# A three-block layer on one core: where the low parts of plain gate weights come from, and five reorderings beside it

## The chip, the core and the metric

The kernel runs on one core of a Trainium2 chip. The core has a matmul engine (TensorE, PE in the profile, with its weight loads as PEld), three engines for elementwise work (VectorE = DVE, ScalarE = ACT, GpSimd = POOL), a SyncE (SP) that here only issues DMA transfers, and 16 DMA engines. The metric is the device time of one execution in microseconds (us).

## The reference

One layer of a model over 2048 prompt tokens and 64 sample tokens, all in float32, model width 1024. Cut to what matters:

```python
h = rms_norm(x, g_pre)
vA, bA, cA, zA, q, f, iv, zB, gA, gB = split_cols(h @ w_in)      # ten outputs of 1024 columns
u = cA * vA                                                       # path A
yA = (silu(zA) * bA * causal_conv3(conv_hist ++ u, conv_w)) @ w_a_out
S_new, o = hgrn2_scan(S0, silu(q) * scale, 1 - fg, iv, log(fg))   # path B: 8 heads, chunks of 64
yB = (head_norm(o) * g_onorm * silu(zB)) @ w_b_out
merged = sigmoid(gA) * yA + sigmoid(gB) * yB
x = x + rms_norm(merged @ w_o, g_post)
gate = sigmoid(rms_norm(x, g_ple) @ w_ple_gate)
x = x + (p @ w_ple_proj) * gate
return x, new_conv, S_new
```

## The kernel before

The 2112 tokens are cut into three blocks of 768, 704 and 640 (the sample tokens end block 1), called block 0, 1 and 2 here. A block is worked in two halves of 384, 352 and 320 columns. Activations lie with the 1024 features over 8 row tiles of 128 partitions (k = 0 to 7), tokens along the free axis.

**Precision.** Every operand is split into a high part (a cast, on ACT) and a low part (value minus high part, on DVE; function `split`, L207). A product takes three matmuls: high by high, high by low, low by high. They stand in L382 to L384 for the groups below, in L516 to L518 for `in_turn`, in L549 to L551 for plain products (`mm3`).

**Groups of seven products.** `sgroup` makes two output tiles (128 output columns each, called i1 and i2) for both halves of a block with seven products instead of eight, each over 4 k: 7 x 4 x 3 = 84 matmuls. The products take, in this order, the weights A11, S3, S1, S2, A12, A22, S4 (the table PRODUCTS). A11, A12 and A22 are plain blocks of the weight matrix; S1 to S4 are sums and differences of its blocks. Results pass through banks `pg`; L396 copies a bank to an `hf` tile, L402, L407, L422 and L429 add such pieces on DVE.

**Where weights come from.** Block 0 loads plain blocks (`load_raw`, L217, queue SP), computes the sums on DVE (L316), splits both (L207), and stores the sums (L295) and the low parts (L244, tensor `low`) to DRAM. Blocks 1 and 2 load everything through SP, in program order: for each weight the raw tile (L217), whose high part ACT casts (L237), and the low part (L238). `kept_w` does this for one weight, `combined` for a group. Tiles rotate: 5 of `raw`, 4 of `hi`, 4 of `lo`, 3 of `s`. `low_tile` deals out tiles for loaded lows by a counter: three of seven lie in an `s` tile, four in a `lo` tile. A load waits on SP until the tile that it is to fill has been read by PE, and what is queued behind it on SP waits too.

**Order in a block.** First the groups of the gates gA and gB (`gates`; in blocks 1 and 2 the first seven of them run ahead, woven into the norm at the end of the block before). Then path B (`path_b`): for each of 8 heads two groups (`head_prep`), and pieces of the attention of the head before (`head_attn`, L951 to L1029), which are put in between products through a list of hooks, one taken after each product of a group. Then path A (`path_a`): for j from 0 to 7 two groups each, followed by DVE work such as L808, L827 and L840; at the top of each j it takes a step of a side job (`side`). Then the outputs: block 0 with plain products, blocks 1 and 2 with `in_turn`; W_O of blocks 0 and 1 is made in `final_out` by plain products. Its first two output tiles are made together in `gemm_late`: for each tile and half, all k but one (`late`: 7 in block 0, 3 in block 1), then the late k of all four. Last come the norm (`final_norm`) and the operands of the next block.

**The side job for sums.** `prepare_sums` makes the four sums of each group of W_O (in block 1) and W_G (in block 2) ahead: it loads four blocks through the POOL queue (L339), computes S1, S3, S2, S4 on DVE (L356, L358, L360, L362), stores each (L345), splits it (L207) and stores its low (L348). From j = 3 on, each j takes one step: the four sums of one group, and then the loads of the next.

**Norms.** `col_rstd` turns sums of squares into a factor per token, for each half: transposes on PE (L640), a reduction on DVE (L642), scale and offset on DVE (L611), a power on POOL (L613); `spread` brings the columns back over all partitions by transposes (L624). `rms` does it for both halves, one after the other.

The order on each engine comes from a scheduler that follows program order with priorities (`tc.high_priority`, `placed` and `behind_all` change it).

Of the kernel before, what the change touches and what calls it, by code (L numbers as in the profile page):

```python
# [83 lines left out]
def hybrid_step(  # L84
# [147 lines left out]
    def split_w(raw, key=None, queue=SP):  # L232

        hi = wp.tile([P, 4, P], F32R, tag="hi", name=nm("hi"))
        if key in lows:
            lo = low_tile()
            A.copy(hi, raw)  # L237
            SP.dma_start(lo.bitcast(F32), lows[key])  # L238
            return hi, lo
# [58 lines left out]
    def kept_w(i1, i2, name, anew=False):  # L298
# [4 lines left out]
        return split_w(load_raw(sums[i1][name]), (i1, name))  # L303

    def combined(i1, i2, first):

        queue = SP if first else G
        with tc.high_priority():
            if not first and i1 in sums:
                return {n: kept_w(i1, i2, n) for _, n, _, _, _ in PRODUCTS}  # L310
            a11, a21, a22, a12 = (load_raw(w_blk[i, h]) for i, h in ((i1, 0), (i2, 0), (i2, 1), (i1, 1)))
            out = dict(A11=split_w(a11, (i1, 0), queue))
# [10 lines left out]
            out["A12"] = split_w(a12, (i1, 1), queue)  # L323
            out["A22"] = split_w(a22, (i2, 1), queue)
# [3 lines left out]
    def prepare_sums(firsts, ahead):  # L328
# [23 lines left out]
        for n, (i1, _) in enumerate(groups):  # L352
# [3 lines left out]
            V.tensor_tensor(a22, a21, a22, ALU.add)  # L356
            keep("S1", i1, a22)
            V.tensor_tensor(a21, a11, a21, ALU.subtract)  # L358
            keep("S3", i1, a21)
            V.tensor_tensor(a11, a22, a11, ALU.subtract)  # L360
            keep("S2", i1, a11)
            V.tensor_tensor(a12, a12, a11, ALU.subtract)  # L362
            keep("S4", i1, a12)
            if not ahead and n + 1 < len(groups):
                nxt = load(*groups[n + 1])
            yield

    def sgroup(i1, i2, hc, sink, first, mid=None, by_k=False):
# [17 lines left out]
        if by_k:  # L386
            for k in range(KH):
                for n in range(4):
                    product(n, (k,))
# [41 lines left out]
    def plain_group(i1, i2, hs, sink, raws=None, between=None):  # L431
# [4 lines left out]
        def split_of(c, h):  # L436
            key = ((i1, i2)[c], h)
            raw = raws[c, h] if raws else load_raw(w_blk[key])
            with nullcontext() if raws else tc.high_priority():
                w[c, h] = split_w(raw, key)  # L440
# [126 lines left out]
    def gemm_late(idxs, act, segs, late):  # L567
# [3 lines left out]
        ks = [k for k in range(KB) if k != late] + [late]  # L571
# [44 lines left out]
    def cols_tile(n):  # L616
        return small.tile([P, (n + P - 1) // P], F32, tag=f"cols{n}", name=nm("cols"))
# [16 lines left out]
    def col_rstd(acc, n):  # L634

        pc = ps_attn()
        cols = cols_tile(n)
        with placed():
            for i, o in tiles_of(n):
                T.transpose(pc[:, i * P : i * P + P], acc[:, o : o + P], ident)  # L640
        nt = cols.shape[1]
        V.tensor_reduce(cols, cols3(pc, nt), axis=mybir.AxisListType.X, op=ALU.add)  # L642
        rstd_of(cols, cols, 1.0 / D)
        return cols

    def rms(acc, out, segs, copy=A.copy):


        cols = [col_rstd(acc[:, cols_of(sg)], sg["n"]) for sg in segs]
# [881 lines left out]
```

## Time and profile before

| | us |
|---|---|
| median of three runs | 2614.24 (2612.5 to 2616.74) |
| the profiled execution | 2618.3 |
| its span | 2616.6 |
| TensorE busy | 2584.3 (99%) |
| VectorE busy | 1648.8 (63%) |
| ScalarE busy | 1525.9 (58%) |
| GpSimd busy | 376.6 (14%) |
| moved by DMA | 747.01 MB, 285 GB/s in the mean |

How to read it. A busy share counts the time in which an instruction of the engine is under way, so 99% on PE does not say that PE runs at its peak: matmuls are pipelined, and a late operand or a lower granted clock shows in how many start in a stretch. A group's row gives line, engine, operation, tiles (output, then inputs), count, busy time and mean of one in ns, then the idle time ahead and what ended it. In the list of waits a row says which line stood, for what, how long in all, how often, and the longest. Times in windows count from the start of the span. Block 0 lasts until about 900 us, block 1 until about 1760; path B of block 2 lies between about 1900 and 2150, its path A from about 2150 to 2305.

### The profile page before, as it was taken

The page shows a single profiled execution, that of the slowest core. Times are in us where ns is not written, and L with a number is a line of the kernel's source. Part 1 is how long each engine was busy: PE and PEld are TensorE (multiplying, and loading weights), DVE is VectorE, ACT ScalarE, POOL GpSimd, SP SyncE. Part 2 cuts the span into 40 slices and gives each one's busy share as a digit, 9 for nine tenths or more (in the row PEclk, how much of TensorE's full clock was granted, in tenths as well). Part 3 has the DMA queues.
Part 4 walks back from the last instruction along what each step waited for, and adds up shares of the span by engine and source line. Part 5 has one row for each costly group of instructions (what it writes and reads, how often), then busy time and mean ns, then how long its engine had stood idle before and what let it go on. Part 6 is the DMA issues. An engine that isn't in the chain of part 4 may idle for free.

```text
span 2616.6 us, 47076 instructions
## 1 busy us (share of the span) xinstructions
PE 2584.3 (99%) x16432; PEld 2564.4 (98%) x16432; DVE 1648.8 (63%) x3165; ACT 1525.9 (58%) x2908; POOL 376.6 (14%) x698
## 2 busy tenths in 40 slices
PE   8999999999999999999999999999999999999999
PEld 8999999999999999999999999999999999999999
DVE  8687788788757655445554557845344444568776
ACT  6666576554433564567775546546677755556746
POOL 1000000110144021210011221002100000211110
PEclk9999999999999999999999999999999999999999
DMA  7677677788788698876768998859977779999977
GB/s 274 220 262 265 232 247 263 274 302 268 267 330 286 233 379 284 279 242 223 229 224 296 364 381 304 305 167 377 366 252 244 245 254 332 381 335 359 344 264 264
DMA packets 362095, 747.01 MB, mean 285 GB/s; under 512 B 44513, under 2 KB 49153, under 8 KB 361857
## 3 DMA queue, kind: packets, MB, share of 16 engines
q1 hardware_dynamic: 319680, 579.81, 64.2%
q0 software_dynamic: 41888, 164.15, 17.2%
q8 instruction: 129, 2.11, 0.3%
q14 instruction: 110, 0.89, 0.1%
q10 hardware_dynamic: 288, 0.05, 0.0%
HBM read 532.26 MB, written 211.57 MB: 284 GB/s over the span
## 4 chain that ended last, share of the span: by engine, by line
PE 82%; DMA 5%; ACT 4%; DVE 3%; issue 2%; POOL 1%; ACTq 0%; POOLq 0%; SPq 0%; DVEq 0%
PE pg L382 16%; PE pg L383 16%; PE pg L384 16%; PE pg L551 5%; PE pg L550 5%; PE pg L549 5%; PE pg L516 4%; PE pg L517 4%; PE pg L518 3%; DMA raw<-S 2%; DMA r<-w_blk 1%; PE pa L984 1%; PE pa L1020 1%; PE pa L970 1%; ACT hi L237 1%
## 5 line engine op out<-in xcount | busy, mean ns | idle before, releaser
L382 PE MATMUL pg<-r,hi 128*128 128x320 f32 (+2 forms) x3304 | 1087.5, 329 | 5.5 <-DVE r L429 3.8
L383 PE MATMUL pg<-r,hi 128*128 128x320 f32 (+2 forms) x3304 | 1069.3, 324 | 0.0
L384 PE MATMUL pg<-r,lo 128*128 128x384 f32 (+2 forms) x2356 | 766.9, 326 | 4.1 <-DMA lo<-low 4.1
L237 ACT CAST hi<-raw 128x512 fp32r<-128x512 f32 x720 | 442.9, 619 | 465.5 <-PE pg L383 137.2
L382 PEld LDWEIGHTS pg<-r,hi 128*128 128x128 f32 x3304 | 622.6, 188 | 7.9 <-issue 4.7
L383 PEld LDWEIGHTS pg<-r,hi 128*128 128x128 f32 x3304 | 622.7, 188 | 0.2 <-DVE r L207 0.2
L384 PEld LDWEIGHTS pg<-r,lo 128*128 128x128 f32 x2356 | 443.2, 188 | 5.1 <-DMA lo<-low 5.1
L384 PE MATMUL pg<-r,s 128*128 128x352 f32 (+1 forms) x948 | 299.3, 316 | 1.0 <-DMA s<-low 1.0
L549 PE MATMUL pg<-r,hi 128*128 128x384 f32 (+1 forms) x768 | 256.1, 334 | 1.6 <-ACT r L207 1.6
L550 PE MATMUL pg<-r,hi 128*128 128x384 f32 (+1 forms) x768 | 256.1, 334 | 0.1
L207 ACT CAST hi<-raw 128x512 fp32r<-128x512 f32 x218 | 134.7, 620 | 178.2 <-PE pg L550 57.9
L207 DVE TENSOR_TENSOR r<-r,r 128x320 fp32r<-128x320 f32 (+7 forms) x298 | 182.0, 633 | 64.9 <-ACT r L207 63.9
L551 PE MATMUL pg<-r,lo 128*128 128x384 f32 (+1 forms) x656 | 219.9, 335 | 0.0
L517 PE MATMUL pg<-r,hi 128*128 128x320 f32 (+1 forms) x672 | 211.1, 316 | 0.2 <-DVE r L207 0.2
L516 PE MATMUL pg<-r,hi 128*128 128x320 f32 (+1 forms) x672 | 206.0, 316 | 0.9 <-ACT r L207 0.8
L207 DVE TENSOR_TENSOR lo<-raw,hi 128x512 fp32r<-128x512 f32 x218 | 149.3, 686 | 63.1 <-ACT hi L207 60.4
L207 ACT CAST r<-r 128x320 fp32r<-128x320 f32 (+7 forms) x298 | 161.0, 576 | 46.0 <-DVE r L715 12.7
L207 ACT CAST hi<-s 128x512 fp32r<-128x512 f32 x160 | 98.0, 618 | 145.7 <-PE pg L383 130.8
L384 PEld LDWEIGHTS pg<-r,s 128*128 128x128 f32 x948 | 178.5, 188 | 1.8 <-DMA s<-low 1.8
L396 ACT COPY hf<-pg 128x352 f32<-128x352 f32 (+2 forms) x354 | 156.7, 444 | 3.8 <-PE pg L384 3.6
L207 DVE TENSOR_TENSOR lo<-s,hi 128x512 fp32r<-128x512 f32 x160 | 110.1, 689 | 68.9 <-ACT hi L207 67.3
L549 PEld LDWEIGHTS pg<-r,hi 128*128 128x128 f32 x768 | 144.8, 189 | 2.2 <-ACT r L207 2.2
(365 smaller groups left out, 4097.7 us busy)
## 6 DMA issues: line engine op xcount, KB each, us to landing
raw<-w_blk SPq DMA_DIRECT2D x570, 256.0 KB, 4.2
lo<-low SPq DMA_DIRECT2D x411, 256.0 KB, 4.6
raw<-S SPq DMA_DIRECT2D x408, 256.0 KB, 4.4
low<-lo SPq DMA_DIRECT2D x314, 256.0 KB, 3.5
s<-low SPq DMA_DIRECT2D x309, 256.0 KB, 4.5
S<-s SPq DMA_DIRECT2D x152, 256.0 KB, 3.2
r<-w_blk POOLq DMA_DIRECT2D x64, 256.0 KB, 6.8
S<-r POOLq DMA_DIRECT2D x64, 256.0 KB, 5.8
```

The costliest lines, as they stand in the source:

```text
L207: return A.copy(hi, src).ins, V.tensor_tensor(lo, src, hi.bitcast(F32), ALU.subtract).ins
L237: A.copy(hi, raw)
L382: add(hi[:, k, :], xhi, start=start and k == 0, stop=False)
L383: add(hi[:, k, :], xlo, start=False, stop=False)
L384: last[0] = add(lo[:, k, :], xhi, start=False, stop=k == KH - 1).ins
L396: copied = A.copy(got[n], ps[bank])
L516: add(hi[:, k, :], xhi, start=start and k == 0, stop=False)
L517: add(hi[:, k, :], xlo, start=False, stop=False)
L518: last[0] = add(lo[:, k, :], xhi, start=False, stop=k == KH - 1).ins
L549: T.matmul(ps, hi[:, k % 4, :], xhi[:, c], start=k == ks[0], stop=False)
L550: T.matmul(ps, hi[:, k % 4, :], xlo[:, c], start=False, stop=False)
L551: last[0] = T.matmul(ps, lo[:, k % 4, :], xhi[:, c], start=False, stop=k == ks[-1]).ins
```

## The change

It has six parts.

1. In blocks 1 and 2 the low parts of plain blocks (A11, A12, A22) in the groups are no longer loaded: DVE makes them from the loaded raw tile (L207 gets 240 more instructions of 128x512), in `lo` tiles. Block 0 no longer stores them. On SP, lows loaded fall from 720 to 480 (240 fewer), lows stored from 314 to 192 (122 fewer). The lows of S1, S2 and S3 always take an `s` tile; that of S4 is still dealt by the counter.
2. `prepare_sums` for W_O and W_G stops after each sum. For j above 3, the steps run as hooks in path A, at every third product, so that the sums come between the products of a j, not at its top.
3. The first two output tiles of W_O in block 1 take k in the order 4, 5, 6, 7, 0, 1, 2 and then 3 (before 0, 1, 2, 4, 5, 6, 7, then 3). Block 0's order is the same as before.
4. In the first gate group of a block, the four products that go by k run as (A11, S3) for k 0 and 1, (S1, S2) for k 0 and 1, then all four for k 2 and for k 3. Before, all four ran for each k.
5. `col_rstd` takes both halves at once: one L611 and one L613 of six columns instead of two of three.
6. In path B of block 2 the attention pieces of a head start one product later (one more empty hook).

The number of matmuls is the same. Cut to its core:

```diff
-    def split_w(raw, key=None, queue=SP):
+    def split_w(raw, key=None, queue=SP, spare=None):
         hi = wp.tile([P, 4, P], F32R, tag="hi", name=nm("hi"))
         if key in lows:
-            lo = low_tile()
+            lo = low_tile() if spare is None else sum_tile(F32R)
...
-    def kept_w(i1, i2, name, anew=False):
+    def kept_w(i1, i2, name, anew=False, spare=None):
...
-        return split_w(load_raw(sums[i1][name]), (i1, name))
+        return split_w(load_raw(sums[i1][name]), (i1, name), spare=spare)
...
-                return {n: kept_w(i1, i2, n) for _, n, _, _, _ in PRODUCTS}
+                return {n: kept_w(i1, i2, n, True, None if n == "S4" else True) for _, n, _, _, _ in PRODUCTS}
...
-            out["A12"] = split_w(a12, (i1, 1), queue)
-            out["A22"] = split_w(a22, (i2, 1), queue)
+            out["A12"] = split_w(a12)
+            out["A22"] = split_w(a22)
...
+            for name, dst, x, y, op in steps:
+                V.tensor_tensor(dst, x, y, op)
+                keep(name, i1, dst)
+                if name == "S4" and not ahead and n + 1 < len(groups):
+                    nxt = load(*groups[n + 1])
+                if name == "S4" or not ahead:
+                    yield
...
         if by_k:
-            for k in range(KH):
-                for n in range(4):
-                    product(n, (k,))
+            for ns, ks in (((0, 1), (0, 1)), ((2, 3), (0, 1)), ((0, 1, 2, 3), (2,)), ((0, 1, 2, 3), (3,))):
+                for k in ks:
+                    for n in ns:
+                        product(n, (k,))
...
-        ks = [k for k in range(KB) if k != late] + [late]
+        ks = [(late + 1 + k) % KB for k in range(KB)]
...
-        cols = [col_rstd(acc[:, cols_of(sg)], sg["n"]) for sg in segs]
+        cols = col_rstd([acc[:, cols_of(sg)] for sg in segs])
...
-            hooks.extend([None] * 3 if first and hd == 0 else [])
+            hooks.extend([None] * (3 if first and hd == 0 else 1 if bl["last"] else 0))
...
-                if j >= 3:
+                if j == 3:
                     next(sums_, None)
+                elif j > 3 and not first:
+                    hooks.extend([partial(next, sums_, None), None, None] * 4)
```

How the order moves, at three places. PE at the start of W_O in block 1, before (r_4682 is the high part of row 0, r_4683 its low part, r_4689 row 1, r_4696 row 2, r_4755 row 4; L624 are the last transposes of the norm factors):

```order
L624 MATMUL pa_4825_20458<-ident_75,cols_3954_16592 128x128 x3
L549 MATMUL pg_4838_20487<-r_4682_19816,hi_4827_20465 128x352
L550 MATMUL pg_4838_20487<-r_4683_19817,hi_4827_20465 128x352
L551 MATMUL pg_4838_20487<-r_4682_19816,s_4828_20466 128x352
L549 MATMUL pg_4838_20487<-r_4689_19848,hi_4827_20465 128x352
L550 MATMUL pg_4838_20487<-r_4690_19849,hi_4827_20465 128x352
L551 MATMUL pg_4838_20487<-r_4689_19848,s_4828_20466 128x352
L549 MATMUL pg_4838_20487<-r_4696_19880,hi_4827_20465 128x352
```

and now (r_4630 is row 4, r_4637 row 5, r_4644 row 6):

```order
L627 MATMUL pa_4700_20205<-ident_75,cols_3829_16339 128x128 x3
L552 MATMUL pg_4713_20234<-r_4630_19885,hi_4705_20218 128x352
L553 MATMUL pg_4713_20234<-r_4631_19886,hi_4705_20218 128x352
L554 MATMUL pg_4713_20234<-r_4630_19885,s_4706_20219 128x352
L552 MATMUL pg_4713_20234<-r_4637_19914,hi_4705_20218 128x352
L553 MATMUL pg_4713_20234<-r_4638_19915,hi_4705_20218 128x352
L554 MATMUL pg_4713_20234<-r_4637_19914,s_4706_20219 128x352
L552 MATMUL pg_4713_20234<-r_4644_19943,hi_4705_20218 128x352
```

The second half of the weight tile and the rows 4 to 7 come first; rows 0 to 2 follow after 12 matmuls.

DVE in path A of block 2, at the second of the four groups of W_G's sums, before (L407 to L429 are a group's additions; L356 to L362 the four sums; L808 path A's own work):

```order
L407 TENSOR_TENSOR hf_27064<-hf_27064,hf_27079 128x320
L402 TENSOR_TENSOR hf_27049<-hf_27049,pg_27081 128x320
L429 TENSOR_TENSOR r_26990<-hf_27049,hf_27064 128x320
L356 TENSOR_TENSOR r_26984<-r_26983,r_26984 128x512
L358 TENSOR_TENSOR r_26983<-r_26982,r_26983 128x512
L360 TENSOR_TENSOR r_26982<-r_26984,r_26982 128x512
L362 TENSOR_TENSOR r_26985<-r_26985,r_26982 128x512
L429 TENSOR_TENSOR r_26990<-hf_27049,pg_27051 128x320
L808 TENSOR_TENSOR r_26991<-pg_27036,r_26990 128x320
```

and now (the four sums share line L363; L405, L410 and L432 are L402, L407 and L429 of before; the L207 with `raw` is a new split of a plain block's low):

```order
L410 TENSOR_TENSOR hf_26939<-hf_26939,hf_26954 128x320
L363 TENSOR_TENSOR r_26966<-r_26965,r_26966 128x512
L405 TENSOR_TENSOR hf_26924<-hf_26924,pg_26972 128x320
L363 TENSOR_TENSOR r_26965<-r_26964,r_26965 128x512
L207 TENSOR_TENSOR lo_27038<-raw_27035,hi_27037 128x512
L432 TENSOR_TENSOR r_26868<-hf_26924,hf_26939 128x320
L363 TENSOR_TENSOR r_26964<-r_26966,r_26964 128x512
L363 TENSOR_TENSOR r_26967<-r_26967,r_26964 128x512
L432 TENSOR_TENSOR r_26868<-hf_26924,pg_26926 128x320
L845 TENSOR_TENSOR r_26693<-r_26693,r_26868 128x640
```

The sums stand in the second group of a j now, spread among the additions; before, they stood in its first group, all four between two additions.

SP in block 2, before, the loads of a group's weights (S1, S2, A12, A22, S4 by name or `w_blk`; each raw tile is followed by the low of the weight before it):

```order
L238 DMA s_6401_27493<-low_1937_7718 128x512
L217 DMA raw_6405_27502<-S2_1944_7732 128x512
L238 DMA lo_6404_27499<-low_1942_7728 128x512
L217 DMA raw_6408_27508<-w_blk 128x512
L238 DMA s_6407_27505<-low_1947_7738 128x512
L217 DMA raw_6411_27514<-w_blk 128x512
L238 DMA lo_6410_27511<-low_1950_7744 128x512
L217 DMA raw_6414_27520<-S4_1955_7754 128x512
L238 DMA s_6413_27517<-low_1953_7750 128x512
```

and now, in another group of block 2 (s_6385, s_6388 and s_6391 take the lows of this group's S3, S1 and S2; lo_6361 takes the low of the S4 of the group before):

```order
L217 DMA raw_6383_27721<-S3_1951_8005 128x512
L217 DMA raw_6386_27727<-S1_1956_8015 128x512
L238 DMA s_6385_27724<-low_1954_8011 128x512
L217 DMA raw_6389_27733<-S2_1961_8025 128x512
L238 DMA s_6388_27730<-low_1959_8021 128x512
L217 DMA raw_6392_27739<-w_blk 128x512
L238 DMA s_6391_27736<-low_1964_8031 128x512
L238 DMA lo_6361_27588<-low_1930_7877 128x512
L217 DMA raw_6395_27745<-w_blk 128x512
L217 DMA raw_6398_27751<-S4_1970_8043 128x512
```

Only sums have lows to load, and the S4 low of a group stands behind the S2 low of the next.

46 lines of the change are left out of this document (21 added, 25 removed).

## The prediction

> **What bounds the kernel now.** I read the page first, then the busy time by stretches, then what TensorE waited for in each stretch, then the landing times of the transfers.
>
> ```profile
> span 2616.6 us, 47076 instructions
> PE 2584.3 (99%) x16432; PEld 2564.4 (98%) x16432; DVE 1648.8 (63%) x3165; ACT 1525.9 (58%) x2908; POOL 376.6 (14%) x698
> ```
>
> TensorE (PE) is the bound, and the change leaves its number of matmuls as it is. So all that can be won is time in which PE stands or runs slowly, and all that can be lost is new time of that kind. How much there is shows in matmuls started per stretch (the columns are length, then busy time with count of PE, weight loads, DVE, ACT and POOL, then granted clock, DMA share, GB/s):
>
> ```profile
> 500.00:700.00 200.00, 200.00 (x1144) 200.00 (x1144) 164.15 (x274) 97.49 (x187) 17.11 (x35) 1.00 0.84 283
> 1480.00:1560.00 80.00, 79.39 (x493) 79.12 (x492) 44.04 (x81) 41.61 (x82) 19.90 (x47) 1.00 1.03 382
> 1760.00:1830.00 70.00, 65.92 (x437) 64.40 (x437) 37.82 (x63) 44.34 (x85) 15.82 (x27) 0.98 0.99 369
> 2150.00:2200.00 50.00, 50.00 (x344) 50.00 (x343) 19.02 (x33) 24.85 (x47) 2.81 (x8) 1.00 0.93 314
> 2230.00:2300.00 70.00, 65.55 (x431) 64.38 (x430) 36.64 (x63) 33.57 (x67) 16.22 (x34) 0.98 1.04 394
> ```
>
> Undisturbed, a matmul of block 2 (320 columns) starts every 50/344 = 0.145 us; one of block 1 (352 columns) about every 79.4/493 = 0.161 us. At 0.145 us, 482 fit into 70 us. Path A of block 2 (2230 to 2300) has 431, so it loses 51 x 0.145 = 7.4 us; the change from block 1 to 2 (1760 to 1830) has 437 and loses 6.5 us. Both have the DMA share at about 1; the first row, at 0.84 and with DVE busy 82% of the time, loses nothing.
>
> The clock takes part in these losses:
>
> ```profile
> 1698.10:1701.54 3.44, 1.72 (x7) 0.94 (x6) 3.26 (x8) 1.25 (x4) 0.54 (x1) 0.99 0.92 324
> 1701.54:1704.95 3.41, 3.41 (x13) 3.20 (x12) 2.52 (x6) 0.98 (x2) 0.00 (x0) 0.51 0.10 41
> ...
> 1800.50:1803.90 3.40, 1.34 (x9) 1.34 (x10) 1.55 (x3) 0.95 (x2) 1.08 (x2) 1.00 1.03 405
> 1803.90:1807.35 3.45, 3.45 (x15) 3.45 (x14) 1.88 (x3) 2.93 (x5) 0.54 (x1) 0.51 1.04 413
> ...
> 2260.50:2264.00 3.50, 2.20 (x15) 1.94 (x14) 0.00 (x0) 0.62 (x1) 0.00 (x0) 1.00 1.04 410
> 2264.00:2267.50 3.50, 3.10 (x22) 2.84 (x20) 3.09 (x5) 1.25 (x2) 1.66 (x4) 1.00 1.05 392
> 2292.00:2295.46 3.46, 1.62 (x12) 1.39 (x11) 3.32 (x7) 0.62 (x1) 2.17 (x4) 0.99 1.06 393
> 2295.46:2298.87 3.41, 3.41 (x14) 3.41 (x14) 2.23 (x3) 2.85 (x6) 0.18 (x1) 0.51 1.03 405
> ```
>
> Three times a stretch in which PE was busy for only 1.3 to 1.7 of 3.4 us is followed by one at a granted clock of 0.51, with 13 to 15 matmuls where 21 to 24 fit: 1.2 to 1.4 us lost each, 3.9 us in all. A stretch with 2.20 us busy was followed by full clock. So I take it that a wait costs about 1.3 us more once two of them fall close together.
>
> The Trainium skill, "TensorE: Matmul & The Clock Gate", section "HAM oscillation — how this bites in real kernels", sets the bar higher: PE idle for more than about 3.4 us on end. Here the longest waits before the three stretches are near 2 us, so the trace disagrees; by that rule the 3.9 us would not go away with the waits, and the time forecast below would be about 3.9 us longer.
>
> **The change, part by part.**
>
> *W_O of block 1 from k 4 on.* The first output pair reads its left half for all k but one, then its right half. What PE waited for from 1690 to 1900:
>
> ```profile
> PE pg L384 <- DMA lo<-low: 2.2, 1, 2.2
> PE pg L549 <- ACT r L207: 1.6, 2, 1.2
> PE pg L382 <- ACT hf L396: 0.9, 1, 0.9
> PE pg L384 <- DMA s<-low: 0.5, 1, 0.5
> ```
>
> The L549 waits lie at 1698.10 to 1704.95: right halves of the merged rows 0 to 2, which are split last. 20 matmuls started there where 43 fit: 3.7 us lost, 1.3 of it by clock. Starting at k 4 puts 12 matmuls (12 x 0.161 = 1.9 us) ahead of the first late row. The last of the three rows comes some 3.5 us after the first is asked for, so not every wait goes, but what is left is too short for the clock to drop. I take 2.6 us, between 1.2 (waits halved, the clock still drops) and 3.7.
>
> *Plain gate blocks split on chip.* For each of 80 groups in blocks 1 and 2, three loads of a low (256 KB) are replaced by three splits on DVE: 240 loads fewer, and 122 stores in block 0 that are no longer needed. The stores lie where PE loses nothing (500 to 700), so they bring nothing. What a split costs:
>
> ```profile
> L207 DVE TENSOR_TENSOR lo<-raw,hi 128x512 fp32r<-128x512 f32 x218 | 149.3, 686 | 63.1 <-ACT hi L207 60.4 <-DMA low<-lo 1.2 <-ACT r L207 0.9
> ```
>
> 240 x 0.686 = 165 us of DVE, 2.06 us in a group of 84 x 0.145 = 12.2 us: DVE in path A of block 2 goes from 52% to 69%, less than the 82% of 500 to 700. There the same splits ran and PE stood nowhere. I cost them at nothing in steady stretches; their cover is the weights being loaded several products early, and if it is gone a split shows with up to 0.7 us. At the first gate group of a block, where a weight is wanted at once, I charge 0.3 us.
>
> The load on DMA falls by three of 14 weight transfers per group, 3 x 0.262 MB / 12.2 us = 64 GB/s: from 394 to about 330 in path A of block 2. How long a 256 KB transfer takes at such loads, in order 1755 to 1780, 2150 to 2200 (314 GB/s by its row above), 2200 to 2300 and 2300 to 2400 (name, queue, count, size, median us from issue to landing):
>
> ```profile
> DMA packets 3360, 7.00 MB, mean 280 GB/s; under 512 B 404, under 2 KB 404, under 8 KB 3358
> lo<-low SPq DMA_DIRECT2D x7, 256.0 KB, 4.3
> ...
> lo<-low SPq DMA_DIRECT2D x17, 256.0 KB, 3.8
> ...
> DMA packets 18213, 37.91 MB, mean 379 GB/s; under 512 B 2303, under 2 KB 2303, under 8 KB 18206
> lo<-low SPq DMA_DIRECT2D x30, 256.0 KB, 6.8
> ...
> DMA packets 16202, 34.28 MB, mean 343 GB/s; under 512 B 2010, under 2 KB 2026, under 8 KB 16191
> raw<-S SPq DMA_DIRECT2D x29, 256.0 KB, 5.2
> ```
>
> Between 3.8 at 314 and 5.2 at 343 lies 4.6 us at 330: my value, with 3.8 and 6.8 as ends.
>
> *Where the sums' lows lie.* The lows of S1, S2, S3 now always take one of three "s" tiles, S4's one in three groups of seven. After such an S4, the low of the next group's S2 can be issued only when S4's product is done, three products (3 x 12 x 0.145 = 5.2 us, 5.8 in block 1) ahead of its use; 4.6 fits. But SP issues in order. Where S4's low goes to a "lo" tile and is queued behind such an S2, which happens four times in path A of block 2, about 4.0 us are left for it: 4 x 0.6 = 2.4 us lost. At the first gate group of block 2, S1 and S2 wait for tiles that W_O's last lows hold, leaving 3.0 and 3.4 us against 4.3 (first row above): 1.3 + 0.9, of which the second is partly covered by the first; 1.7. Before, each low had six products. This part costs 4.1 us, between 0 and 30 (the slower rival).
>
> *With these, the waits for lows at the change of block.* Of the 6.5 us lost from 1760 to 1830, 9 + 15 matmuls in 1800.50 to 1807.35, where 47 fit, are 3.3 us: one wait of 2.2 for a low and the clock after it. That low is one of a plain block or lies behind them; I take 3.0, with -1 and 5 as ends.
>
> *First gate group in two pairs, one power per norm.* What PE waited for from 896 to 986, the change from block 0 to 1:
>
> ```profile
> PE pg L382 <- ACT hi L237: 0.7, 1, 0.7
> PE pg L384 <- DMA lo<-low: 0.7, 1, 0.7
> PE pa L624 <- POOL cols L613: 0.5, 1, 0.5
> PE pg L384 <- DMA s<-low: 0.5, 1, 0.5
> ```
>
> Taking (A11, S3) for two k before S1 and S2 gives those two weights 12 matmuls instead of 6, 1 us. I take 0.9 of the 1.9 us of weights. The powers:
>
> ```profile
> L613 POOL TENSOR_TENSOR cols<-cols,mhalf 128x3 f32<-128x3 f32 x14 | 14.3, 1028 | 49.7 <-DVE cols L611 49.7
> L613 POOL TENSOR_TENSOR cols<-cols,mhalf 128x1 f32<-128x1 f32 x12 | 8.0, 668 | 47.5 <-DVE cols L611 47.3
> ```
>
> One column 0.67 and three 1.03 give 0.18 a column, so six take about 1.6 against 2 x 1.03 at worst; at most 0.5 us for each norm on the path, with the first half waiting longer and the second less. I take 0.3 for block 0 to 1 and 0.3 for the others; ends -1 and 1.
>
> *One more hook before attention in block 2.* From 1900 to 2150 PE waited seven times (there are eight heads); behind it, one of them in order of time:
>
> ```profile
> PE pa L953 <- DVE r L429: 2.0, 7, 0.3
> ```
>
> ```profile
> 2023.27 0.60 PE L951 MATMUL pa<-ident,r 128*128 128x128 f32 x4
> 2024.19 0.84 PE L953 MATMUL pa<-ident,r 128*128 128x128 f32 x4 [0.33 <-DVE r L429]
> ```
>
> L953 starts 0.92 us after four matmuls that are done in 0.60, and its own four take 0.24 longer than those: 0.3 bare wait, up to 0.32 + 0.24 = 0.6 lost. The attention comes one product (1.74 us) later, more than the wait. DVE now has splits in front of L429, at most three (2.06 us) and mostly one. I take 0.5 x 7 = 3.5 us; ends 0 and 4.2.
>
> *Sums one by one.* Four loads, four sums: before, the loads are issued at one j and DVE stands on them at the top of the next. From 2230 to 2300 on DVE and 2190 to 2300 on PE:
>
> ```profile
> DVE r L356 <- DMA r<-w_blk: 17.8, 3, 6.4
> ```
>
> ```profile
> PE pg L382 <- DVE r L429: 3.2, 3, 1.8
> PE pg L384 <- DMA lo<-low: 1.3, 1, 1.3
> ```
>
> Behind the four sums stands L429, which frees the bank that PE wants. DVE waits of 5 to 6.4 us reached PE with 0.8 to 1.8; so some 4.3 us of it were hidden. Now the sums come half a j later and other work stands between them: the loads have 5 to 6 us, 2 to 3 more than before, and what wait is left on DVE stays under what is hidden. Gone are 3.2 of waits, 1.4 of clock and the restart after each: 5.0 of the 7.4 us; ends 0 and 7.4. In block 1 there is one such wait, 0.3.
>
> **Sum.** 2.6 + 3.0 + 0.9 + 0.6 + 3.5 + 5.0 + 0.3 = 15.9 won, 0.3 + 4.1 lost: 11.5 us net. The profiled execution took 2618.3 us (span 2616.6), which is 4.1 above the median of the runs, 2614.24. 2618.3 - 11.5 - 4.1 = 2602.7, so 2603.
>
> **Rivals.**
>
> *Slower: the short leads meet slow transfers.* If the DMA stays as full as now (it may: what is no longer asked for lets other loads start earlier) and a low takes 6.8 us, it is late by 1.6 in seven groups of path A of block 2, by 1.0 in seven of block 1, by 2.8 for the four S4: 11 + 7 + 11 us; the first gate group adds 2, beyond the 1.7 charged: 31 lost, 2.4 of it charged already. Against this, the 11.5: about 17 us slower, 2631; with 6.2 us in place of 6.8 some 7 slower. It decides from a landing time of about 5.9 us on. For it: 1.04 is a full queue, and 394 GB/s may be what the queue gives, not what is asked. Against it: the 343 GB/s of 2300 to 2400 went with 5.2. 0.17.
>
> *About the same.* A landing time of some 5.3 us costs the S4 lows 3 us more and the first gate group 2; DVE, still late with a sum, keeps 3 of the 5.0 us. Gain 3 to 4: 2611. 0.16.
>
> *More.* All waits named go with their clock, the lows come in time: 3.7 + 5 + 1.9 + 1 + 4.2 + 7.4 - 4 (what else is lost at the change of block and in path A, for which I have no cause) = 19: 2595. For it: landing at 3.8 if 314 GB/s is reached. 0.17.
>
> *Splits and powers in each other's way.* POOL's power could be held up by the added DVE work: then the two norms at the changes of block lose up to 0.69 each and the gains there halve, 3 us less: 2606, inside the forecast's range. The Trainium skill, "SBUF — State Buffer", section "Who interferes with whom", says that a DVE instruction with two SBUF inputs, which a split is, contends with a GpSimd instruction that reads SBUF. From 500 to 700, with DVE at 82%, nothing of PE's time was lost; the rows do not show a held-up power.
>
> **How the numbers follow.** My forecast has 0.50, 2598 to 2608. What a measurement of this kernel can tell from no change is about 0.2%, 5.2 us. Below 2609 lie the forecast and the larger gain: 0.67 faster; 0.16 the same; 0.17 slower. The range from 2593 to 2615 holds the first two and most of the "same" case; outside are the slower rival and a little on either side.
>
> **What the profile after would show.** W_O right: L549 waits under 1 us and no 0.51 near 1702. Sums right: no wait for L429 in path A of block 2, DVE waits on its sums under 4 us each. Hook right: no L953 row. Splits right: DVE near 1810 us, lows in path A landing in 4 to 5 us, DMA share below 1. New waits of L384 for s<-low or lo<-low, over 6 us in sum, or landing times still above 6, would make the prediction wrong; so would splits that PE waits for (L384 <- DVE lo L207).

## The result

The changed kernel is slower: 2631.19 us in the median against 2614.92 of the kernel before, a ratio of 1.0063 with a 95% interval from 1.0044 to 1.0082. The forecast was 2603, with a range from 2593 to 2615. The profiled execution of the changed kernel took 2627.35 us, the fastest of its four; that of before, with 2618.3, lay above its median. So the two traces lie 9 us apart, and the medians 16.

The page of the changed kernel, its span and its busy times:

```profile
span 2625.7 us, 46666 instructions
PE 2581.0 (98%) x16432; PEld 2564.6 (98%) x16432; DVE 1795.0 (68%) x3400; ACT 1528.5 (58%) x2908; POOL 378.3 (14%) x693
```

The number of matmuls is the same, DVE has 146 us more, and PE stands longer. What it waited for, whole execution, the first four rows:

```profile
PE pg L386 <- DMA lo<-low: 16.5, 5, 5.1
PE pg L386 <- DMA s<-low: 7.3, 6, 2.7
PE pa L1089 <- ACT r L207: 6.9, 1, 6.9
PE pa L627 <- POOL cols L616: 3.2, 5, 1.4
```

(L386 is L384 of before, L627 is L624.) Waits for lows were 4.1 + 1.0 us; they are 16.5 + 7.3. The waits for L429's sums, for W_O's operands (L549) and for the attention (L953) are gone. By stretches (896 to 986 is the change from block 0 to 1, 1690 to 1712 the start of W_O in block 1, 1760 to 1830 the change from block 1 to 2, 1900 to 2150 path B and 2190 to 2320 path A of block 2, 2230 to 2300 a part of it; the columns are those of the prediction's tables of stretches):

```profile
896.00:986.00 90.00, 88.61 (x551) 87.67 (x551) 63.48 (x95) 56.51 (x103) 16.82 (x28) 1.00 0.87 305
1690.00:1712.00 22.00, 21.75 (x137) 21.44 (x136) 10.41 (x24) 9.18 (x20) 1.08 (x2) 1.00 0.70 243
...
1760.00:1830.00 70.00, 61.87 (x418) 59.97 (x417) 45.81 (x74) 42.48 (x81) 13.58 (x22) 1.00 0.88 313
1900.00:2150.00 250.00, 250.00 (x1822) 249.82 (x1821) 155.13 (x345) 175.56 (x329) 22.77 (x35) 1.00 0.63 197
2230.00:2300.00 70.00, 60.78 (x385) 60.26 (x384) 40.80 (x69) 33.39 (x63) 16.57 (x34) 0.90 0.83 281
...
2190.00:2320.00 130.00, 114.76 (x740) 113.73 (x739) 74.32 (x125) 61.12 (x117) 24.13 (x50) 0.93 0.84 286
```

The rows of the kernel before that the prediction did not show:

```profile
896.00:986.00 90.00, 87.21 (x539) 85.49 (x538) 51.27 (x77) 55.22 (x102) 17.73 (x30) 1.00 0.97 354
1690.00:1712.00 22.00, 20.28 (x114) 19.10 (x114) 11.24 (x26) 5.85 (x12) 1.07 (x2) 0.92 0.61 216
1900.00:2150.00 250.00, 247.96 (x1785) 244.74 (x1785) 123.65 (x294) 175.13 (x324) 22.48 (x35) 1.00 0.75 245
...
2190.00:2320.00 130.00, 125.55 (x841) 124.38 (x840) 65.88 (x113) 66.93 (x132) 27.32 (x59) 0.99 1.02 379
```

W_O and path B lose nothing now. At the change of block 418 matmuls started where 437 did, 19 x 0.145 = 2.8 us worse. In path A of block 2, from 2230 to 2300, it is 385 against 431, 6.7 us worse, at a clock of 0.90 in the mean. From 2190 to 2320, which takes in all the long waits, it is 740 against 841: 101 x 0.145 = 14.6 us worse. The waits there:

```profile
PE pg L386 <- DMA lo<-low: 15.2, 4, 5.1
```

These four are the four S4 lows of the prediction's SP order. The third of them, as SP issued it and as PE took it:

```profile
2269.12 0.73 SPq L238 DMA_DIRECT2D s<-low  x1
2269.94 0.56 SPq L217 DMA_DIRECT2D raw<-w_blk  x1
2270.84 0.32 SPq L238 DMA_DIRECT2D s<-low  x1
2271.20 0.71 SPq L238 DMA_DIRECT2D lo<-low  x1
```

```profile
2279.82 0.63 PE L386 MATMUL pg<-r,lo 128*128 128x320 f32 x1 [5.07 <-DMA lo<-low]
```

Issued at 2271.20, wanted at 2279.82 - 5.07 = 2274.75: a lead of 3.55 us, near the 4.0 of the prediction. It landed after 8.6. The landing times from 2200 to 2300:

```profile
raw<-S SPq DMA_DIRECT2D x27, 256.0 KB, 3.6
s<-low SPq DMA_DIRECT2D x23, 256.0 KB, 3.7
raw<-w_blk SPq DMA_DIRECT2D x21, 256.0 KB, 4.3
...
lo<-low SPq DMA_DIRECT2D x3, 256.0 KB, 7.7
```

So in the median over this stretch transfers did become as quick as forecast (4.6), or quicker. Around the third wait, from 2262 to 2282, they were not:

```profile
q0 software_dynamic: 853, 2.81, 39.1%
...
raw<-w_blk SPq DMA_DIRECT2D x4, 256.0 KB, 8.1
s<-low SPq DMA_DIRECT2D x4, 256.0 KB, 7.0
raw<-S SPq DMA_DIRECT2D x4, 256.0 KB, 6.7
r<-w_blk POOLq DMA_DIRECT2D x4, 256.0 KB, 5.7
...
lo<-low SPq DMA_DIRECT2D x1, 256.0 KB, 8.6
```

The first row (packets, MB, share) is what the POOL queue moved: 2.81 of 6.54 MB. It is the side job: it issued the four loads of its next group (r<-w_blk) from 2265.5 to 2267.1, and then stored sums and lows. The second and the fourth low were issued as near behind such loads, the first was not; all four had a lead of about 3.5 us:

| issued at | side job's loads issued | landed after | wait of PE |
|---|---|---|---|
| 2213.6 | none after 2184.9 | 4.8 | 1.3 |
| 2239.7 | 2234.0 to 2235.6 | 7.7 | 4.2 |
| 2271.2 | 2265.5 to 2267.1 | 8.6 | 5.1 |
| 2302.9 | 2297.1 to 2298.7 | 8.2 | 4.7 |

Three stretches around the second wait show what it does:

```profile
2243.40:2246.20 2.80, 0.00 (x0) 0.00 (x0) 2.73 (x6) 0.97 (x2) 1.36 (x4) 0.99 1.06 411
2246.20:2249.60 3.40, 2.19 (x8) 2.20 (x9) 0.64 (x2) 0.00 (x0) 0.54 (x1) 0.50 1.04 412
2249.60:2253.00 3.40, 3.40 (x15) 3.40 (x14) 1.85 (x3) 1.09 (x2) 0.54 (x1) 0.50 0.54 169
```

While PE stands the DMA engines are full (411 GB/s, where the mean of this part is 281): the low shares them with what SP issued around it and with the side job. Then come 6.8 us at half clock.

### The profile page after: what moved, and what is told of

It is laid out like the page before. It is cut to its first block, busy times and chain, and to the rows that moved or that the text cites. A ratio compares the mean times of both kernels' runs of the same rounds, so it can differ in the third digit from the quotient of the medians.

```text
span 2625.7 us, 46666 instructions
## 1 busy us (share of the span) xinstructions
PE 2581.0 (98%) x16432; PEld 2564.6 (98%) x16432; DVE 1795.0 (68%) x3400; ACT 1528.5 (58%) x2908; POOL 378.3 (14%) x693
## 4 chain that ended last, share of the span: by engine, by line
PE 86%; issue 5%; DMA 4%; POOL 1%; DVE 1%; ACT 0%; SPq 0%; POOLq 0%; ACTq 0%; DVEq 0%
PE pg L384 19%; PE pg L386 19%; PE pg L385 19%; PE pg L520 4%; PE pg L519 4%; PE pg L521 4%; PE pg L553 3%; PE pg L554 3%; PE pg L552 3%; DMA lo<-low 2%; PE pa L989 1%; PE pa L1025 1%; PE pa L1027 1%; PE pa L975 1%; DMA s<-low 1%
## 5 line engine op out<-in xcount | busy, mean ns | idle before, releaser
L384 PE MATMUL pg<-r,hi 128*128 128x320 f32 (+2 forms) x3304 | 1088.9, 330 | 1.7 <-ACT hf L399 0.9
L386 PE MATMUL pg<-r,lo 128*128 128x384 f32 (+2 forms) x2232 | 730.5, 327 | 16.6 <-DMA lo<-low 16.5
L384 PEld LDWEIGHTS pg<-r,hi 128*128 128x128 f32 x3304 | 623.2, 189 | 3.4 <-ACT hf L399 1.2
L207 ACT CAST hi<-raw 128x512 fp32r<-128x512 f32 x458 | 282.1, 619 | 293.1 <-issue 70.8
L386 PEld LDWEIGHTS pg<-r,lo 128*128 128x128 f32 x2232 | 421.6, 189 | 18.4 <-DMA lo<-low 18.3
L207 DVE TENSOR_TENSOR lo<-raw,hi 128x512 fp32r<-128x512 f32 x458 | 313.7, 687 | 151.7 <-ACT hi L207 147.6
L386 PE MATMUL pg<-r,s 128*128 128x320 f32 (+1 forms) x1072 | 338.2, 315 | 7.3 <-DMA s<-low 7.3
L207 DVE TENSOR_TENSOR r<-r,r 128x320 fp32r<-128x320 f32 (+7 forms) x298 | 182.5, 633 | 48.9 <-ACT r L207 48.1
L386 PEld LDWEIGHTS pg<-r,s 128*128 128x128 f32 x1072 | 201.3, 188 | 9.2 <-DMA s<-low 9.2
L207 ACT CAST r<-r 128x320 fp32r<-128x320 f32 (+7 forms) x298 | 161.7, 576 | 46.1 <-DVE r L720 12.7
L207 ACT CAST hi<-s 128x512 fp32r<-128x512 f32 x160 | 98.0, 618 | 144.8 <-PE pg L385 132.3
L207 DVE TENSOR_TENSOR lo<-s,hi 128x512 fp32r<-128x512 f32 x160 | 110.2, 690 | 64.1 <-ACT hi L207 64.0
```

Of the source, the lines that this page charges most:

```text
L207: return A.copy(hi, src).ins, V.tensor_tensor(lo, src, hi.bitcast(F32), ALU.subtract).ins
L384: add(hi[:, k, :], xhi, start=start and k == 0, stop=False)
L386: last[0] = add(lo[:, k, :], xhi, start=False, stop=k == KH - 1).ins
```

## The experiments

Ratios are to the kernel before, run on the same chip in the same job, with 95% intervals. "Position" below means how many raw weight loads stand on SP between a sum's raw tile and its low. In the kernel before it is 1 for nearly all of them. In the changed kernel S4's lows in `lo` tiles have position 3 in 34 of 59 cases, and 5 or 6 in five; four of the five are the four waits above. So the place of these four is the same, though their waits run from 1.3 to 5.1 us.

**S4's low always in a `lo` tile.** Theory A was that S4's low in an `s` tile does the harm, since it makes the next S2 low wait.

```diff
-            lo = low_tile() if spare is None else sum_tile(F32R)
+            if spare is None:
+                lo = low_tile()
+            elif spare:
+                lo = sum_tile(F32R)
+            else:
+                lo = wp.tile([P, 4, P], F32R, tag="lo", name=nm("lo"))
...
-  kept_w(i1, i2, n, True, None if n == "S4" else True)
+  kept_w(i1, i2, n, True, n != "S4")
```

> The changed kernel, but S4's low always takes a lo tile, so that three s tiles serve three lows a group and no low waits for the end of the group before. Theory A (the tiles: an S4 low in an s tile makes the next S2 low wait, and the next S4 low stands behind it on SP): the four waits for lo<-low in path A of block 2 (15.2 us in the changed kernel) and the half-clock stretches after them go, the wait for the first gate group of block 2 stays; some 18 to 20 us faster than the changed kernel, about 2610 to 2613. Theory B (the transfers come in bursts since the sums are spread, so that a low takes 8 us wherever it is queued): at least half of the waits stay, 2620 or more.

It took 2648.75 us, 1.0126 [1.0106, 1.0145]. Waits for lows:

```profile
PE pg L391 <- DMA lo<-low: 36.1, 15, 7.0
```

Theory A falls: without S4 in `s` tiles there are more waits. Position 5 or 6 occurs 14 times now, and there are 15 waits. That points to where a low that goes to a `lo` tile stands on SP; the run on ACT's queue below tests it.

**All sums' lows dealt by the counter.**

```diff
-  kept_w(i1, i2, n, True, None if n == "S4" else True)
+  kept_w(i1, i2, n, True, None)
```

> The changed kernel, but all lows of sums are dealt to s and lo tiles by the counter, as before the change; plain lows still split on chip. Theory A: the pattern of waits depends on which low falls where; lows in a ring of four lo tiles shared with three splits a group get shorter or longer leads, so waits move to other products but do not vanish, total PE waits for lows 5 to 20 us, 2608 to 2625. Theory B: waits in path A of block 2 as in the changed kernel, near 15 us.

2609.11 us, 0.9974 [0.9965, 0.9983]: faster than before. `lo` tiles mean position 3 here, `s` tiles 0, and 5 is rare.

```profile
PE pg L386 <- DMA lo<-low: 9.3, 7, 3.4
```

With the same splits on DVE, the one expression that gives S1 to S3 `s` tiles is worth 22 us.

**The sums four at a time again.** In the changed kernel, `prepare_sums` and its calls as before the change.

> The changed kernel with the sums for W_O and W_G made as before the change, four at the top of a j. Theory A: the waits for lo<-low in path A of block 2 stay at 12 to 16 us, since their place on SP is the same; the waits behind the sums on DVE come back in part (up to 3 us): 2628 to 2634, no faster than the changed kernel. Theory B: the waits for lows go down to under 5 us: 2615 to 2620.

2634.7 us, 1.0074 [1.0061, 1.0087].

```profile
PE pg L384 <- DMA lo<-low: 13.7, 7, 3.9
```

10.2 us of it lie from 2190 to 2320 (15.2 with the sums one by one), and the total is no better: waits for lows in `s` tiles are 12.6 us, 7.3 in the changed kernel. The time lies just above what theory A expected, and the 10.2 us lie between the two theories. The side job's loads go out at other moments here, and the four lows land after 4.7 to 5.7 us, no longer after 4.8 to 8.6; but three of them are issued only 1.9 to 3.1 us ahead of their use, where it was 3.5. So the half of theory B that concerns the landing time holds, and it is not enough to take the waits away.

**Four of the parts alone.** The kernel before with the orders of W_O and of the first gate group, the one power, and the hook.

> The kernel before with four of the six parts: W_O's k from 4 on, the first gate group in pairs, one power for both halves, one more hook in block 2; no split on chip, no sums one by one. By the traces of before and of the changed kernel: W_O 3.7 us, block 0 to 1 2.1 us, path B of block 2 4.9 us won, the rest as before: 10.7 us faster than the kernel before, about 2604 (theory A, the losses are all with the lows). If the split on chip was what cleared path B of block 2 or W_O (less DMA), the gain is 5 us or less, 2609 or more.

2611.23 us, 0.9984 [0.9974, 0.9993]: 4.7 us in the median, of 10.7 expected. In its trace (span 2606.9):

```profile
896.00:986.00 90.00, 87.49 (x542) 86.05 (x541) 50.84 (x75) 56.04 (x103) 16.84 (x28) 1.00 0.97 357
1690.00:1712.00 22.00, 21.15 (x130) 20.34 (x129) 12.43 (x28) 7.54 (x18) 1.08 (x2) 1.00 0.70 248
1900.00:2150.00 250.00, 250.00 (x1819) 249.81 (x1818) 126.11 (x297) 176.93 (x330) 22.33 (x35) 1.00 0.78 249
```

Without any split on chip path B is clear (1819 matmuls, and 1785 before). W_O has 130, 114 before: 16 x 0.161 = 2.6 us; the changed kernel reaches seven more. The change from block 0 to 1 has 542, 539 before and 551 in the changed kernel: the first gate group in pairs and the one power bring almost nothing there by themselves. The change from block 1 to 2 has 439, 437 before.

**Four `s` tiles, three `lo` tiles.** The lows of all four sums in `s` tiles.

```diff
-  wp.tile([P, 4, P], F32R, tag="lo", name=nm("lo"))
+  wp.tile([P, 4, P], F32R, tag="lo", name=nm("lo"), bufs=3)
-  wp.tile([P, 4, P], dt, tag="s", name=nm("s"), bufs=3)
+  wp.tile([P, 4, P], dt, tag="s", name=nm("s"), bufs=4)
-  kept_w(i1, i2, n, True, None if n == "S4" else True)
+  kept_w(i1, i2, n, True, True)
```

> The changed kernel with four s tiles and three lo tiles instead of three and four; the lows of all four sums lie in s tiles. On SP a sum's low then stands one raw load behind its own raw tile, as in the kernel before, not three to six. Theory C (a low that stands several raw loads behind its own is held on SP by waits for raw tiles, is issued about 4 us before its use, and then shares the DMA engines with all that was held with it): waits for lows in path A of block 2 under 3 us, 2600 to 2607. Rival D (the splits on DVE, now with three lo tiles, are late): waits for lo tiles written by DVE of 5 us and more, 2612 or above.

Theory C was right on path A, and the total was not:

```profile
2230.00:2300.00 70.00, 70.00 (x480) 70.00 (x479) 49.83 (x86) 39.85 (x77) 18.30 (x38) 1.00 1.00 363
```

Nothing is lost there (position 1 in 73 of 90), but the outputs in turn, which take their lows by the counter and now have three `lo` tiles for four, lose it again (9.3 us of this row lie behind 2320):

```profile
PE pg L521 <- DMA lo<-low: 10.3, 10, 3.5
```

2615.78 us, 0.9996 [0.9987, 1.0005].

**Five parts, without the splits on chip.**

> The changed kernel without its first part: lows of plain blocks loaded as before, tiles dealt by the counter; the other five parts kept. If the first part holds all of the loss: faster than the four parts alone by the waits behind the sums on DVE that are left there (4.0 us and a half-clock stretch), 2605 to 2608, no wait for L430's result in path A of block 2. If the sums one by one also cost (their loads and stores among the weights): 2611 or above, with waits for lows in path A of block 2.

2611.46 us, 0.9984 [0.9975, 0.9993], no better than four. From 2190 to 2320 the four parts alone wait thus, first row, and the five parts thus, second fence:

```profile
PE pg L382 <- DVE r L430: 3.4, 3, 2.0
```

```profile
PE pg L386 <- DMA s<-low: 1.7, 2, 1.3
PE pg L386 <- DMA lo<-low: 1.4, 3, 0.6
```

Making the sums one by one does clear the wait behind them; with the full traffic a wait of nearly the size for lows comes in its place, and the median does not move.

**S4's low on chip too.** Only S1 to S3 are loaded; 102 more splits (with those of the outputs in turn, which take S4 by the same function).

```diff
-  return split_w(load_raw(sums[i1][name]), (i1, name), spare=spare)
+  return split_w(load_raw(sums[i1][name]), None if name == "S4" else (i1, name), spare=spare)
```

> The changed kernel, but S4's low is split on DVE as well, so that only S1 to S3 have lows to load, in three s tiles; 80 more splits of 0.69 us on DVE. Theory C: no low stands five loads behind, waits for lo<-low in path A of block 2 vanish, 2602 to 2610. Rival D (DVE as the limit): the splits come late in path B or A, waits for lo tiles from DVE over 5 us, 2615 or above.

2604.59 us, 0.9959 [0.9944, 0.9973].

```profile
2230.00:2300.00 70.00, 70.00 (x478) 70.00 (x477) 52.91 (x91) 40.17 (x77) 18.42 (x38) 1.00 0.95 344
...
1760.00:1830.00 70.00, 68.32 (x466) 67.25 (x466) 54.05 (x86) 46.73 (x90) 16.33 (x27) 1.00 0.90 324
```

No S4 low is loaded, and the loss in path A is gone; DVE, busy for 76% of the time there, holds nobody up. At the change of block 466 matmuls start, 437 before.

**S4's low from ACT's queue.** The sharpest test of the place on SP: same tiles, same bytes, another queue.

```diff
-  SP.dma_start(lo.bitcast(F32), lows[key])
+  (A if key[1] == "S4" else SP).dma_start(lo.bitcast(F32), lows[key])
```

> The changed kernel with one thing moved: S4's low is issued from ACT's queue, not SP's; tiles and bytes are the same. Theory C: what held it was its place on SP; the 15.2 us of waits for lo<-low in path A of block 2 fall below 4, 2608 to 2615. Theory B (bursts on the DMA engines, whatever the queue): landing times of these lows stay near 8 us and the waits above 8, 2620 or above.

From 2190 to 2320, where it was 15.2:

```profile
PE pg L386 <- DMA lo<-low: 0.3, 1, 0.3
```

Their landing times from 2200 to 2320:

```profile
lo<-low ACTq DMA_DIRECT2D x6, 256.0 KB, 6.1
```

Still long against the others; with the 3.55 us that they had from SP the median one would be 2.5 late. But from ACT they are issued some 7.1 us ahead of their use (one at 2241.5, its first matmul at 2248.6). So it was the lead that the place on SP left them, and this half of theory C is shown. Its other half, that they land late because they share the DMA engines with all that was held with them, is not: issued from ACT, held by nothing on SP, the three that go out with the side job's loads (2241.5, 2266.2, 2290.8) still take 6.9 to 7.6 us, as theory B had it for the landing time; the other three take 3.3 to 5.4. No run takes the side job away, so its part in the landing time rests on these comparisons within the traces. The total missed its forecast, 2623.08 us, 1.0037 [1.0025, 1.005]: the waits for `s` tiles at the changes of block stay and grow,

```profile
PE pg L386 <- DMA s<-low: 10.2, 7, 2.7
```

which moving S4 alone does not touch.

**S4 on chip, the sums four at a time.**

> The kernel of the run with S4's low split on chip, with the sums for W_O and W_G made four at a time again, as before the change. If the sums one by one are worth something once no low is late: waits for L432's result behind the sums come back in path A of block 2, 3 to 5 us and a half-clock stretch, 2608 to 2612. If not (fewer transfers alone are enough for the loads of the sums to be in time): 2603 to 2606.

2605.93 us, 0.9961 [0.9947, 0.9976], the same as with the sums one by one. From 2230 to 2320 DVE still stands on its loads, by less than in the kernel before (17.8, longest 6.4), and from 2190 to 2320 PE waits for nothing:

```profile
DVE r L356 <- DMA r<-w_blk: 7.5, 2, 4.0
```

**S4 on chip, six raw tiles** (and 46 tiles in the large ring for 47).

> The kernel of the run with S4's low split on chip, with six raw tiles instead of five (and 46 instead of 47 tiles in the large ring). If raw tiles that wait for DVE and ACT still hold the queue at the changes of stage (W_O, the outputs in turn): waits there shrink by 2 to 4 us, 2600 to 2603. If not, or if the smaller ring makes activations wait: 2604 to 2612.

2627.23 us, 1.0041 [1.0026, 1.0055]. From 985 to 1110, where the run that it was built on has no wait, the first two rows:

```profile
PE pg L554 <- DVE lo L207: 7.9, 3, 3.7
PE pg L386 <- DVE lo L207: 6.1, 3, 3.5
```

Which of the two does it, the smaller ring or the sixth raw tile, was not separated; the question that the run was to answer stays open.

**S4 and two tiles of the final gate on chip.**

```diff
-  pss = gemm(W_G + j, h2, segs)
+  pss = gemm(W_G + j, h2, segs, queue is SP and j < 2)
```

> The kernel of the run with S4's low split on chip; besides, the first two weight tiles of block 1's final gate (W_G, worked in the middle of block 2's end) are split on chip too, not loaded. In that run four lows were issued one right behind the other at 2465.7 us there, after a wait of 6.0 us on SP, and PE waited 2.6 us and had two half-clock stretches. If those loads are the cause: 3 to 5 us faster than that run, about 2600. If DVE is the limit there: 2604 to 2608.

2603.79 us, 0.9949 [0.9936, 0.9961], the best of all, though within the noise of the run it was built on. The wait for a low in the final gate (2.6 us) is gone, and waits for the norm's power grow from 3.5 to 5.7 us.

**The kernel before with splits on chip alone**, S4's among them.

> The kernel before with only the first part, in the form that held best: plain blocks' lows and S4's split on chip, S1 to S3 loaded into s tiles; none of the other five parts. By the stretches of the traces it gains path A of block 2 (some 5 to 6 us) and the change from block 1 to 2 (2 to 4), and leaves W_O (4.2 us less what fewer transfers give) and path B of block 2 (5.0 us) as before, if DVE's added splits do not make its waits longer: 2606 to 2611. If the added splits do lengthen the waits for L429's result in path B: 2612 or more.

2610.07 us, 0.9976 [0.9967, 0.9986]. Path B keeps its waits, somewhat longer:

```profile
PE pa L953 <- DVE r L429: 2.8, 7, 0.5
```

So the splits in front of L429 do add a little (2.0 before), and only the hook takes the wait away. The changes of block and W_O, which keep their old order here, are another matter:

```profile
896.00:986.00 90.00, 88.74 (x551) 87.51 (x550) 67.46 (x103) 56.53 (x103) 17.45 (x30) 1.00 0.83 288
1690.00:1712.00 22.00, 21.66 (x137) 21.34 (x136) 12.47 (x29) 10.77 (x24) 1.06 (x2) 1.00 0.63 212
...
1760.00:1830.00 70.00, 68.63 (x467) 67.35 (x466) 53.91 (x88) 46.78 (x89) 16.94 (x29) 1.00 0.90 324
```

551 and 137 matmuls are what the changed kernel has as well, so the splits alone take these losses away, without the pairs in the first gate group and without the new order of k. At the change from block 1 to 2 it is 467, as in the run with S4 on chip and all other parts (466). In path A of block 2, from 2230 to 2300, it is 462, against 431 before and 478 there.

6.3 us from the splits here and 4.7 from the four parts make 11.0, and the two runs that have both gained 11.1 (sums one by one) and 10.5 (four at a time). That the sum comes out is no proof that the gains are separate: at W_O the two cure the same wait.

## Why the prediction was wrong

**W_O: right on the wait, not needed beside the splits.** 2.6 us were taken; by counts it is 2.6 with the order alone, and (137 - 114) x 0.161 = 3.7 in the changed kernel, the upper end. The half-clock stretch at 1702 is gone. But the splits alone, with the old order, reach the same 137, which the prediction did not see: it took it that the right halves of the merged rows come late whatever the other parts do. Why they come earlier with the splits was not traced.

**First gate group in pairs: counted twice in the same way.** 0.9 us were taken at the change from block 0 to 1. The stretch does gain 12 matmuls, 12 x 0.161 = 1.9 us, but three of them with the four parts alone and all 12 with the splits alone.

**The hook: right in kind, low in size.** 3.5 us were taken, with 4.2 as the upper end; 37 more matmuls start in path B, 37 x 0.137 = 5.1 us (250/1822 = 0.137). L953's waits are all gone, and come back where the hook is missing.

**Sums one by one: right on the wait, wrong on its worth.** 5.0 us were taken. The waits for the sums' additions do go, but without the splits other waits replace them (four parts against five parts, no difference), and with the splits and S4 on chip four sums at a time do as well. The term was counted as this part's own; it came with the lighter traffic.

**One power: no gain.** 0.6 us were taken. Six columns are quicker than twice three, 1.92 us against 2.40 at the first norm, and 1.36 in the other four uses, where the prediction worked out 1.6:

```profile
24.02 1.92 POOL L616 TENSOR_TENSOR cols<-cols,mhalf 128x6 f32<-128x6 f32 x1 [1.00 <-DVE cols L614]
```

But PE's waits for powers went from 1.8 us to 3.2; the first half now waits for both.

**Splits on DVE at no cost: right in these stretches.** 1822 matmuls start in path B with DVE at 62%, and 478 in path A with DVE at 76% (S4 on chip). With six raw tiles PE did wait for splits, 7.9 and 6.1 us.

**Splits and powers in each other's way: real, but not made worse.** The powers of four columns took 1078 ns in the mean in the changed kernel and 1076 before, but the mean hides two of the 24, in both kernels. Those two began while DVE was at work on inputs that all lie in SBUF, and took 1.45 and 1.61 us where the other 22 took about 1.04. One of them, 0.17 us after DVE had begun an L832 of 0.88 us:

```profile
1377.94 1.61 POOL L616 TENSOR_TENSOR ms<-ms,mhalf 128x4 f32<-128x4 f32 x1 [1.41 <-DVE ms L614]
```

So "the rows do not show a held-up power" was read off a mean. No power of four columns in blocks 1 and 2 began beside one of the added splits, and those of six columns at the changes of block took their 1.36 us, so this rival cost nothing here.

**Landing time: right in the median, wrong for the four that mattered.** This is the step that failed: "Where S4's low goes to a "lo" tile and is queued behind such an S2, which happens four times in path A of block 2, about 4.0 us are left for it: 4 x 0.6 = 2.4 us lost." The place and the number of cases were right and the lead nearly so (3.5 us); the landing time was taken as 4.6 us, read off the mean load of a long stretch. But the load is not even: where the side job's transfers run beside SP's the DMA engines are full (405 to 414 GB/s in the three long waits), and what SP issues in those microseconds takes 6 to 9 us. Three of the four lows fell into such a time and landed after 7.7, 8.6 and 8.2 us; the first, which did not, landed after 4.8. The term measured 15.2 us of waits, and the clock added to it (6.8 us at half speed at the second wait, as shown, and stretches at the third and the fourth too): 14.6 us lost by counts in path A, where 5.0 - 2.4 = 2.6 us were to be won. That makes some 17 of the 28 us between forecast and result. The first gate group and the change of block, 2.0 lost against 3.0 won, came out at 2.8 lost: two waits for `s` tiles of over 2 us each.

**What no term held.** The medians lie 7 us further apart than the traces: 3.4 us because the trace of before was slow for its kernel, 3.8 because that of the changed kernel was fast. The granted clock of the executions says something of the second part: 0.997 in the profiled one, 0.995 in the two that took 2632.88 and 2635.23 us. 0.002 x 2626 is about 5 us, an estimate, of the 5.5 and 7.9 us between them, so more of the half-clock stretches seem to account for most of it; what those executions waited for, no trace shows.

**The rival that it came to** was named: slower by short leads, 2631, at 0.17. That its figure is the measured one is luck. Its mechanism for S4 (2.8 us late each) is the one that the traces show, 3.8 in the mean. Its other terms are not: the lows in `s` tiles of path A, with three products of lead, were in time (0 us where 11 were put down). Its condition, a landing time of about 5.9 us or more, was met in the bursts, where three of the four S4 lows stood, and not by the median, which is where the weighing went wrong: the evidence against it (343 GB/s with 5.2 us) spoke of means.

**The rule on the clock.** The prediction took it that waits which leave PE busy for half of a 3.4 us stretch already bring one at half clock. Where the waits went (W_O, and path A with S4 on chip), the half-clock stretches went with them, so they belong to those waits, the longest of which were 1.2 and 1.8 us. Such a wait does not always bring one: with the four parts alone PE waits 2.0 us in path A, and the clock there stays at 1.00. These waits are shorter than the idle stretch of about 3.4 us of the Trainium skill, "TensorE: Matmul & The Clock Gate", section "HAM oscillation — how this bites in real kernels"; the waits of 4.2 to 5.1 us in the changed kernel pass that mark, and the one shown brought two such stretches.

## What to carry to other kernels

Price a transfer by two things: the lead that its place in the issuing queue leaves it, and the landing time in the few microseconds in which it is issued, with what other queues send then; a median over a long stretch hides both. Removing loads from a queue that is worked in order moves the rest of them too; look for each remaining load at what it now stands behind, and test that by issuing it from another queue. And where two edits cure the same wait, run each alone before giving both a term in the sum.

## What was not expected

- Taking 95 MB of transfers away (747 to 652) made the kernel slower, and splitting one more low of each group on DVE (71% busy then) made it 26.6 us faster (2631.19 to 2604.59).
- S4's low always in a `lo` tile cost 17.6 us more than letting the counter deal it. Yet the tile itself is not late: by the order of the matmuls, the tile of such a low had been read seven products (84 x 0.145 = 12.2 us) before its use. Why the scheduler puts these lows so far back on SP was not tried.
- The order of k at W_O and the pairs in the first gate group, each made for a wait that was there, cured waits that the splits cure as well.
